# Two bias tiles of each width in the attention of a decoder trunk, the wide ones in the norms' tiles, and two tiles for the squares of q and k

## The chip, the cores and the metric

The kernel runs on one core of one Trainium2 chip. The metric is the device time of one execution in microseconds (us). The engines are named as the profile names them: PE (TensorE, matmuls), PEld (its weight loads), DVE (VectorE), ACT (ScalarE), POOL (GpSimd) and SP (SyncE, whose queue carries the DMAs of the weights). SBUF is the on-chip memory that all of them read and write, PSUM the banks into which PE accumulates.

## The reference, cut to what matters

The input is one sequence of 512 tokens with 1024 channels, in float32. Two layers run one after the other, each a token mixer with a residual add and then a squared-ReLU MLP with a residual add. The first mixer is a chunked gMLP; the second, around which the change lies, is an attention with 16 heads of 64 channels, normalised q and k, a forget-gate bias on the logits and a sigmoid gate on its output:

```
p = h @ w_in
q, k, v, gate, f_logit = split(p)
q = rms_norm(q, q_g);  k = rms_norm(k, k_g)            # per head
c = cumsum(log_sigmoid(f_logit + b_f), axis=tokens)    # per head
for each block i of 128 query rows, keys 0 .. (i+1)*128:
    logits = q @ k.T * Dh**-0.5 + c[query] - c[key]
    logits = where(query >= key, logits, -inf)
    o = softmax(logits) @ v
o = o * sigmoid(gate)
out = o @ w_out
```

For one head the four query blocks have 128, 256, 384 and 512 keys. The term `c[query] - c[key]`, with the causal mask in it, is what the kernel calls the bias.

## The kernel before, in words

The channels lie on the 128 partitions and the 512 tokens along the free axis. Every float32 matrix product is made of three matmuls with split operands (high by high, high by low, low by high), so each weight chunk comes from DRAM into a tile `raw`, ACT copies its high part `wh` (L85), and DVE, or POOL while the attention runs, subtracts it to get the low part `wl` (L86). The chunks are numbered (wl122 is the low part of chunk 122); `Stream` loads and splits them some chunks ahead of PE.

The stages follow each other: gMLP, first MLP, attention (from 638.6 to 934.5 us of the profiled span), second MLP. In the attention, eight pairs of heads are projected (`project`), one or two q/k/v column groups at a time, and the work of a pair's softmax (`attend(p, y)`, one generator per pair) is woven between the projection's matmuls. The order on PE is pinned by the program (`FOX_ORDER` says in which order projections, gates and output products come, and the `LAG_...` constants say how many microseconds of PE work lie between the steps of a generator). On DVE, ACT, POOL and SP the order is made when the kernel is built, by a scheduler with a time model, which sees when each tile comes free.

A pair's way, with the lines that the profile names: its q and k stand in `y`; ACT squares them into `ysq` (L725, two halves of 512), DVE sums the squares (L726), POOL raises them to -0.5 (L728, `yss`), DVE multiplies (L729). Then for each head `hd` of the pair a row of `c` is brought to all partitions (`cb`, L788), and for each of the four widths:

- POOL makes the bias tile from `cb` and `ct` (L795, `tensor_scalar`) and masks its diagonal block (L797, `affine_select`). The order listing calls the tile of head 9 and width 512 `bias9_3`.
- PE makes the logits `lg`, DVE adds the bias into `ee` and takes the row minimum `mn` (L806), ACT takes the exponential and its row sums (L807).

After the four, DVE takes the reciprocal `rc` of the sums (L809) and multiplies the four `ee` by it (L811, four instructions). PE turns `ee` into `tp`, ACT and DVE make its high and low parts `pth` (L845) and `ptl` (L846), and PE multiplies them with the values `v` into `ot` (one PSUM bank, shared by all heads). `v` comes from the projection's PSUM through ACT (L679) and DVE (L680). ACT and DVE bring `ot` into `oz` (L829, L830) and multiply it by the gate (L831); `output` multiplies `oz`'s halves with the output weights and adds the result to the residual stream `x` (L327).

Before the change each bias width has one tile, in the pool `fp`, so head `hd+1`'s bias of a width can be made once head `hd`'s L806 of that width has read it. `ysq` has one tile too. The pool `small` holds, for the four norms of the trunk, the tiles `sq` and `sqs` (512 wide, two of each; `Norm.square`), which no one uses while the attention's heads run; the norm after the attention squares `x` only at the attention's end.

Of the kernel before, what the change touches and what calls it, by code (L numbers as in the profile page):

```python
# [8 lines left out]
F32 = mybir.dt.float32  # L9
# [7 lines left out]
P = 128  # L17
D = 1024
S = 512
# [5 lines left out]
DH = 64  # L25
# [115 lines left out]
def trunk(ctx: ExitStack, tc: tile.TileContext, A, out, stages=4):  # L141
# [6 lines left out]
    small = ctx.enter_context(tc.tile_pool(name="small", bufs=2))  # L148
# [3 lines left out]
    def psA(name):  # L152
        return ps.tile([P, S], F32, tag="A", name=name, bufs=4)
# [455 lines left out]
    with ExitStack() as st:  # L609
        fs = st.enter_context(tc.tile_pool(name="fs", bufs=2))  # L610
        fp = st.enter_context(tc.tile_pool(name="fp", bufs=2))
# [16 lines left out]
        def forget(pq):  # L628

            fl = fp.tile([P, NT, H], F32, tag="fl", name="fl", bufs=1)  # L630
            for i in range(NT):
                dve.scalar_tensor_tensor(fl[:, i], pq[i][:, 3 * P : 3 * P + H], nm.rstd[:, i : i + 1], bf, op0=ALU.mult, op1=ALU.add)
            ff = fl.rearrange("p i h -> p (i h)")
            fa = fp.tile([P, NT * H], F32, tag="fa", name="fa", bufs=1)
            dve.scalar_tensor_tensor(fa, ff, -1.0, ff, op0=ALU.mult, op1=ALU.min)
            act.activation(fa, fa, AF.Exp)
            act.activation(fa, fa, AF.Ln, bias=1.0)
            dve.scalar_tensor_tensor(ff, ff, 0.0, fa, op0=ALU.min, op1=ALU.subtract)

            pre = fp.tile([P, NT, H], F32, tag="pre", name="pre", bufs=1)  # L640
            dve.memset(pre[:, 0], 0.0)
            for i in range(1, NT):
                dve.tensor_tensor(pre[:, i], pre[:, i - 1], fl[:, i - 1], op=ALU.add)
            yield LAG_FORGET, None
            pc = psD("pc")
            mm(pc[:, : NT * H], tri, ff, True, False)
            mm(pc[:, : NT * H], ones, pre.rearrange("p i h -> p (i h)"), False, True)
            dve.tensor_scalar(ct.rearrange("p i h -> p (i h)"), pc[:, : NT * H], -1.0, None, op0=ALU.mult)
            yield LAG_PT, None
            pt = psD("pct")  # L650
            for i in range(NT):
                turn(pt[:H, i * P : (i + 1) * P], ct[:, i])
            cs = fp.tile([H, S], F32, tag="oz", name="cs")
            act.activation(cs, pt[:H], AF.Copy, scale=-1.0)
            nc.sync.dma_start(cd, cs)
            did.add("F")
# [5 lines left out]
        def columns(pq, n):  # L662
            for c in range(4):
                wh, wl = (t[:, : 2 * n].rearrange("p (k n) -> p k n", k=2) for t in ws.take())
                for i in range(NT):
                    for kk in range(2):
                        k = 2 * c + kk
                        sl = slice(i * P, (i + 1) * P)
                        mm3(pq[i][:, :n], nm.h[k][:, sl], nm.l[k][:, sl], wh[:, kk], wl[:, kk], k == 0, k == KB - 1)
                        yield c, i, kk  # L670
# [23 lines left out]
        def project(p, values=True):  # L694
            pq = [psA(f"pq{p}_{i}") for i in range(NT)]
            for c, i, kk in columns(pq, (3 if values else 2) * P + (H if p == 0 else 0)):
                yield None
                if i < NT - 1 or not kk:
                    continue
                if p == 0 and c == 0:  # L700
                    nm.finish()
                if p == 0 and c == 1:
                    nm.spread()
            if p == 0:
                dve.tensor_scalar(epsr, nm.ms, RMS_EPS, None, op0=ALU.mult)
                running.append([order["us"], forget(pq), None])
                advance(True)
                gates[0] = gate_act(0, gates[0])
                did.add(("G", 0))
            if p:  # L710
                yield ("Q", p - 1)
            if values and p > 2:
                yield ("O", p - 3, 1)
            y = fp.tile([P, NT, 2 * P], F32, tag="y", name=f"y{p}", bufs=1)
            for i in range(NT):
                act.activation(y[:, i], pq[i][:, : 2 * P], AF.Copy)
            if values:
                keep_values(p, pq, 2 * P)
            yf = y.rearrange("p i n -> p (i n)")
            yh = yf.rearrange("p (a d) -> p a d", d=DH)  # L720
            ss = fs.tile([P, NT, 4], F32, tag="yss", name=f"yss{p}")
            sf = ss.rearrange("p i a -> p (i a)")
            for c in range(2):
                sq = fp.tile([P, 8, DH], F32, tag="ysq", name=f"ysq{p}_{c}", bufs=1)
                act.activation(sq.rearrange("p a d -> p (a d)"), yf[:, c * S : (c + 1) * S], AF.Square)  # L725
                dve.tensor_reduce(sf[:, 8 * c : 8 * c + 8], sq, axis=AX.X, op=ALU.add)  # L726
            dve.scalar_tensor_tensor(ss, ss, 1.0 / DH, epsr.unsqueeze(2).to_broadcast([P, NT, 4]), op0=ALU.mult, op1=ALU.add)
            pool.tensor_tensor(sf, sf, mhalf, op=ALU.pow)  # L728
            dve.tensor_tensor(yh, yh, sf.unsqueeze(2).to_broadcast([P, NT * 4, DH]), op=ALU.mult)  # L729
            running.append([order["us"] + LAG_NORM, attend(p, y), None])  # L730

        def gate_act(p, pg):
            gt = fp.tile([P, S], F32, tag="gt", name=f"gt{p}")
            dve.tensor_tensor(gt, pg, nm.rbc, op=ALU.mult)
            act.activation(gt, gt, AF.Sigmoid)
            return gt
# [24 lines left out]
        def attend(p, y):  # L761
# [21 lines left out]
            for e in range(2):  # L783
                hd = 2 * p + e
                yield lag, ("T", p - 1, e) if p else "F"
                lag = 0.0
                cb = fp.tile([P, S], F32, tag="cb", name=f"cb{hd}")
                nc.sync.dma_start(cb, cd[hd].partition_broadcast(P))  # L788
                ees = []
                sm = fs.tile([P, NT], F32, tag="sm", name=f"sm{hd}")  # L790
                mn = fs.tile([P, NT], F32, tag="mn", name=f"mn{hd}")
                for i in range(NT):
                    n = (i + 1) * P
                    bi = fp.tile([P, n], F32, tag=f"bias{i}", name=f"bias{hd}_{i}", bufs=1)
                    pool.tensor_scalar(bi, cb[:, :n], 1.0, ct[:, i, hd : hd + 1], op0=ALU.mult, op1=ALU.add)  # L795
                    dg = bi[:, i * P :]
                    pool.affine_select(dg, dg, pattern=[[-1, P]], compare_op=ALU.is_ge, fill=BIG, base=0, channel_multiplier=1)  # L797
                    yield lag, None
                    lag = LAG_LOGIT * rush
                    ee = fp.tile([P, n], F32, tag=f"ee{i}", name=f"ee{hd}_{i}", bufs=2)  # L800
                    ees.append(ee)
                    lg = psB(f"lg{hd}_{i}")
                    ts_ = slice(i * P, (i + 1) * P)
                    mm(lg[:, :n], qs[e][:, ts_], ks[e][:, :n], True, False)
                    mm(lg[:, :n], qs[e][:, ts_], kl[e][:, :n], False, True)
                    dve.tensor_tensor_reduce(ee, lg[:, :n], bi, 1.0, 3.0e38, op0=ALU.add, op1=ALU.min, accum_out=mn[:, i : i + 1])  # L806
                    act.activation(ee, ee, AF.Exp, bias=mn[:, i : i + 1], scale=-1.0, accum_out=sm[:, i : i + 1])  # L807
                rc = fs.tile([P, NT], F32, tag="rc", name=f"rc{hd}")
                dve.reciprocal(rc, sm)  # L809
                for i in range(NT):  # L810
                    dve.tensor_scalar(ees[i], ees[i], rc[:, i : i + 1], None, op0=ALU.mult)  # L811
                soft.append(ees)
                did.add(("L", p, e))
# [19 lines left out]
            for e in range(2):  # L833
                hd = 2 * p + e
# [4 lines left out]
                for j in range(NT):  # L839
                    n = (NT - j) * P  # L840
# [28 lines left out]
        def advance(force):  # L869

            can = [r for r in running if r[2] is None or r[2] in did]
            due = [r for r in can if r[0] <= order["us"]]
            if not due and force and can:
                due = [min(can, key=lambda r: r[0])]
                order["us"] = max(order["us"], due[0][0])
            if not due:
                return False
            r = due[0]
            try:
                lag, r[2] = next(r[1])  # L880
                r[0] = order["us"] + lag
            except StopIteration:
                running.remove(r)
            return True
# [94 lines left out]
```

## Time and profile before

| | us |
|---|---|
| median of 3 runs | 1291.09 (1291.02 to 1291.13) |
| the profiled execution, its own time | 1290.49 |
| its span in the trace | 1288.8 |
| PE busy in the span | 1263.7 (98%) |
| DVE busy | 887.4 (69%) |
| ACT busy | 631.0 (49%) |
| POOL busy | 503.4 (39%) |

The profiled execution is 0.60 us below the median and has 1.7 us outside the span. The granted clock of PE was 0.994 of full speed over the span. Times below are microseconds from the span's start. "busy" of PE counts its matmuls; a bracket behind a row of a timeline tells how long the engine had been idle and which instruction released it.

### The profile page before, as it was taken

The numbers are of one execution on the slowest core, as the hardware profiler recorded it, in microseconds if no ns is written. First come the engines' busy times: TensorE is split into PE (matmuls) and PEld (weight loads), VectorE is DVE, ScalarE is ACT, GpSimd is POOL, SyncE is SP. The second block draws the span as 40 slices with busy tenths as digits, with TensorE's granted clock in tenths as the row PEclk, the third lists the DMA queues.
The fourth block names the chain that finished last, engine by engine and source line by source line (L and its number), as shares of the span: only waits on it lengthen the run. The fifth ranks groups of instructions, "written<-read, shape, count | busy, mean of one in ns | idle before, by whom it ended". The sixth has DMA issues, their size and how long they took to land.

```text
span 1288.8 us, 18536 instructions
## 1 busy us (share of the span) xinstructions
PE 1263.7 (98%) x7180; PEld 1118.5 (87%) x7180; DVE 887.4 (69%) x1212; ACT 631.0 (49%) x993; POOL 503.4 (39%) x423
## 2 busy tenths in 40 slices
PE   9999999998999999999999999999979999999998
PEld 8888888887999999998899899898869999999987
DVE  7347766688767676765536777777897867676763
ACT  7334333355534343443467687678465434444430
POOL 4209423027423232210657667666284422222200
PEclk9999999998999999999999999999989999999999
DMA  7332323222332333323223222223213333232321
GB/s 249 95 115 82 91 90 85 96 83 70 105 121 85 112 95 102 104 94 95 80 83 99 82 83 74 87 78 106 77 64 116 99 98 107 90 114 83 115 82 66
DMA packets 39608, 124.02 MB, mean 96 GB/s; under 512 B 4816, under 2 KB 5840, under 8 KB 39520
## 3 DMA queue, kind: packets, MB, share of 16 engines
q1 hardware_dynamic: 39232, 122.82, 30.4%
q8 instruction: 56, 0.92, 0.3%
q14 instruction: 32, 0.26, 0.1%
q10 hardware_dynamic: 288, 0.02, 0.0%
HBM read 120.69 MB, written 2.13 MB: 95 GB/s over the span
## 4 chain that ended last, share of the span: by engine, by line
PE 85%; DVE 8%; ACT 2%; POOL 2%; issue 1%; DMA 1%; POOLq 0%; ACTq 0%; DVEq 0%
PE po L245 34%; PE da L245 12%; PE bc L245 9%; PE pq L245 8%; PE pv L245 7%; PE pu L245 7%; DVE xl L273 2%; PE pg L245 2%; PE ot L245 2%; DVE wl L86 1%; DVE ee L811 1%; PE lg L245 1%; PE tp L250 1%; PE sp L428 1%; ACT wh L85 1%
## 5 line engine op out<-in xcount | busy, mean ns | idle before, releaser
L85 ACT ACTIVATE wh<-raw 128x1024 fp32r<-128x1024 f32 (+3 forms) x230 | 219.0, 953 | 276.6 <-PE po L245 86.5
L86 DVE TENSOR_TENSOR wl<-raw,wh 128x1024 fp32r<-128x1024 f32 (+1 forms) x178 | 255.0, 1444 | 50.9 <-ACT wh L85 50.5
L245 PE MATMUL po<-zl,wh 128*128 128x512 f32 x512 | 200.5, 392 | 0.0
L245 PE MATMUL po<-zh,wh 128*128 128x512 f32 x512 | 200.2, 391 | 0.0
L245 PE MATMUL po<-zh,wl 128*128 128x512 f32 x512 | 199.5, 390 | 0.0
L559 DVE TENSOR_TENSOR x<-x,po 128x512 f32<-128x512 f32 x128 | 87.3, 682 | 111.5 <-PE po L245 111.5
L86 POOL TENSOR_TENSOR wl<-raw,wh 128x768 fp32r<-128x768 f32 (+3 forms) x52 | 103.1, 1983 | 124.2 <-ACT wh L85 121.7
L112 POOL TENSOR_TENSOR ssum<-raw 128x512 f32<-128x512 f32 x28 | 40.7, 1453 | 261.1 <-DMA raw<-in_m_dram 242.4
L85 ACT ACTIVATE sh<-ssum 128x1024 fp32r<-128x1024 f32 x56 | 59.4, 1061 | 169.5 <-POOL ssum L113 121.7
L245 PEld LDWEIGHTS po<-zh,wl 128*128 128x128 f32 x512 | 96.2, 188 | 19.6
L245 PEld LDWEIGHTS po<-zh,wh 128*128 128x128 f32 x512 | 96.5, 188 | 18.0
L245 PEld LDWEIGHTS po<-zl,wh 128*128 128x128 f32 x512 | 96.6, 189 | 16.2
L245 PE MATMUL pq<-wh,xh 128*128 128x384 f32 (+2 forms) x256 | 88.4, 345 | 0.0
L412 POOL TENSOR_SCALAR vn<-v,mv,lnr 128x128 f32<-128x128 f32 x64 | 63.3, 1004 | 59.4 <-DVE vl L416 59.3
L245 PE MATMUL pq<-wh,xl 128*128 128x384 f32 (+2 forms) x256 | 83.1, 324 | 0.0
L245 PE MATMUL pq<-wl,xh 128*128 128x384 f32 (+2 forms) x256 | 82.7, 323 | 0.0
L86 DVE TENSOR_TENSOR sl<-ssum,sh 128x1024 fp32r<-128x1024 f32 x56 | 71.5, 1277 | 11.5 <-ACT sh L85 11.5
L114 POOL TENSOR_TENSOR ssum<-raw,ssum 128x512 f32<-128x512 f32 x28 | 39.3, 1404 | 75.7 <-DVE sl L86 75.4
L115 POOL TENSOR_TENSOR ssum<-raw,raw 128x512 f32<-128x512 f32 x28 | 63.5, 2269 | 1.2 <-DVE sl L86 1.2
L245 PE MATMUL da<-th,sl 128*128 128x256 f32 x224 | 63.4, 283 | 0.0
L245 PE MATMUL da<-tl,sh 128*128 128x256 f32 x224 | 63.4, 283 | 0.0
L245 PE MATMUL da<-th,sh 128*128 128x256 f32 x224 | 63.1, 282 | 0.0
(212 smaller groups left out, 3517.9 us busy)
## 6 DMA issues: line engine op xcount, KB each, us to landing
raw<-in_m_dram SPq DMA_DIRECT2D x128, 512.0 KB, 3.6
raw<-in_gw_u_dram SPq DMA_DIRECT2D x16, 512.0 KB, 3.5
raw<-in_gw_o_dram SPq DMA_DIRECT2D x16, 512.0 KB, 3.5
raw<-in_fw_qkv_dram SPq DMA_DIRECT2D x20, 384.0 KB, 3.0
raw<-in_gw_v_dram SPq DMA_DIRECT2D x14, 512.0 KB, 3.8
raw<-in_fw_g_dram SPq DMA_DIRECT2D x8, 512.0 KB, 3.4
cb<-cd SPq DMA_DIRECT2D x16, 256.0 KB, 3.3
raw<-in_fw_o_dram SPq DMA_DIRECT2D x8, 512.0 KB, 3.5
```

What stands on the lines that cost most here:

```text
L85: self.nc.scalar.activation(hi, t, AF.Copy)
L86: eng.tensor_tensor(lo, t, hi.bitcast(F32), op=ALU.subtract)
L112: tt(s12[:, 0], a21, a22, op=ALU.add)
L114: tt(s43[:, 0], a12, s12[:, 1], op=ALU.subtract)
L115: tt(s43[:, 1], a11, a21, op=ALU.subtract)
L245: ins = pe.matmul(dst, a, b, start=start, stop=stop, skip_group_check=more)
L250: placed(pe.transpose(dst, src, ident[: src.shape[0], : src.shape[0]]), 256)
L273: dve.scalar_tensor_tensor(l, x[b], gcol, h.bitcast(F32), op0=ALU.mult, op1=ALU.subtract)
L412: pool.tensor_scalar(vn[:, i], v[i][:, cb * P : (cb + 1) * P], mv[:, i, 0:1], lnr[:, i : i + 1], op0=ALU.subtract, op1=ALU.mult)
L428: pe.matmul(dst, vh[:, 2 * c + i], wide, start=True, stop=False)
L559: dve.tensor_tensor(x[b], x[b], pt, op=ALU.add)
L811: dve.tensor_scalar(ees[i], ees[i], rc[:, i : i + 1], None, op0=ALU.mult)
```

## The change

`ysq` gets two tiles instead of one. The biases of the two narrow widths get two tiles each in the pool `fp`; the biases of the two wide widths leave `fp` and use the norms' `sqs` and `sq` (two of each), cut to the width. The bytes per partition of the pools stay the same in sum (1536 and 2048 leave `fp`; 512, 1024 and 2048 come). The lines behind L794 move down by four, so L795 is L799 in the changed kernel, L806 is L810, L811 is L815.

```
-                sq = fp.tile([P, 8, DH], F32, tag="ysq", name=f"ysq{p}_{c}", bufs=1)
+                sq = fp.tile([P, 8, DH], F32, tag="ysq", name=f"ysq{p}_{c}", bufs=2)
...
-                    bi = fp.tile([P, n], F32, tag=f"bias{i}", name=f"bias{hd}_{i}", bufs=1)
+
+                    if i < 2:
+                        bi = fp.tile([P, n], F32, tag=f"bias{i}", name=f"bias{hd}_{i}", bufs=2)
+                    else:
+                        bi = small.tile([P, S], F32, tag="sqs" if i == 2 else "sq", name=f"bias{hd}_{i}", bufs=2)[:, :n]
                     pool.tensor_scalar(bi, cb[:, :n], 1.0, ct[:, i, hd : hd + 1], op0=ALU.mult, op1=ALU.add)
```

No instruction is added or removed. PE's order and the order of the DMAs on SP stay as they were; the scheduler places work on the other three engines anew. On POOL it differs at the first four heads, at heads 9 and 10, and at the end.

POOL at the attention's start, before: the four biases of head 0, then the weight split wl122, and head 1's biases one by one behind it.

```order
L797 AFFINE_SELECT bias0_0_5952<-bias0_0_5952 128x128
L797 AFFINE_SELECT bias0_1_5966<-bias0_1_5966 128x128
L797 AFFINE_SELECT bias0_2_5989<-bias0_2_5989 128x128
L86 TENSOR_TENSOR wl122_5927<-raw122_5747,wh122_5926 128x768
L797 AFFINE_SELECT bias0_3_6006<-bias0_3_6006 128x128
L795 TENSOR_SCALAR bias1_0_6039<-cb1_6035,ct_5603 128x128
L86 TENSOR_TENSOR wl123_5977<-raw123_5821,wh123_5976 128x768
L797 AFFINE_SELECT bias1_0_6039<-bias1_0_6039 128x128
```

The same place in the changed kernel:

```order
L801 AFFINE_SELECT bias0_0_5952<-bias0_0_5952 128x128
L799 TENSOR_SCALAR bias1_0_6039<-cb1_6035,ct_5603 128x128
L799 TENSOR_SCALAR bias1_1_6053<-cb1_6035,ct_5603 128x256
L799 TENSOR_SCALAR bias1_2_6076<-cb1_6035,ct_5603 128x384
L801 AFFINE_SELECT bias0_1_5966<-bias0_1_5966 128x128
L799 TENSOR_SCALAR bias1_3_6093<-cb1_6035,ct_5603 128x512
L801 AFFINE_SELECT bias0_2_5989<-bias0_2_5989 128x128
L86 TENSOR_TENSOR wl122_5927<-raw122_5747,wh122_5926 128x768
L801 AFFINE_SELECT bias0_3_6006<-bias0_3_6006 128x128
L801 AFFINE_SELECT bias1_0_6039<-bias1_0_6039 128x128
```

All four L799 of head 1 now stand ahead of the masks of head 0's last three biases and of wl122; behind the last row come three more masks of head 1, with one L799 of head 2 among them, and then wl123.

POOL at the attention's end, before: head 15's biases stand among the splits wl158 to wl161.

```order
L86 TENSOR_TENSOR wl158_8660<-raw158_8448,wh158_8659 128x1024
L795 TENSOR_SCALAR bias15_0_8772<-cb15_8768,ct_5603 128x128
L795 TENSOR_SCALAR bias15_1_8786<-cb15_8768,ct_5603 128x256
L797 AFFINE_SELECT bias15_0_8772<-bias15_0_8772 128x128
L795 TENSOR_SCALAR bias15_2_8809<-cb15_8768,ct_5603 128x384
L86 TENSOR_TENSOR wl159_8710<-raw159_8517,wh159_8709 128x1024
L797 AFFINE_SELECT bias15_1_8786<-bias15_1_8786 128x128
L797 AFFINE_SELECT bias15_2_8809<-bias15_2_8809 128x128
L795 TENSOR_SCALAR bias15_3_8826<-cb15_8768,ct_5603 128x512
L86 TENSOR_TENSOR wl160_8794<-raw160_8599,wh160_8793 128x1024
L797 AFFINE_SELECT bias15_3_8826<-bias15_3_8826 128x128
L86 TENSOR_TENSOR wl161_8881<-raw161_8657,wh161_8880 128x1024
```

The same place in the changed kernel:

```order
L86 TENSOR_TENSOR wl156_8520<-raw156_8287,wh156_8519 128x512
L728 TENSOR_TENSOR yss7_8506<-yss7_8506,mhalf_120 128x16
L86 TENSOR_TENSOR wl157_8602<-raw157_8364,wh157_8601 128x512
L86 TENSOR_TENSOR wl158_8660<-raw158_8448,wh158_8659 128x1024
L86 TENSOR_TENSOR wl159_8710<-raw159_8517,wh159_8709 128x1024
L86 TENSOR_TENSOR wl160_8794<-raw160_8599,wh160_8793 128x1024
L86 TENSOR_TENSOR wl161_8881<-raw161_8657,wh161_8880 128x1024
```

Head 15's biases are all made ahead of wl156, and the splits follow each other without a bias between them.

DVE at the attention's end, before: behind the four L811 of head 14 (its row of width 256 of head 15's logits comes first), the values v6 and v7 and head 15's last logits.

```order
L806 ISA ee15_1_8803,mn15_8771<-lg15_1_8804,bias15_1_8786 128x256
L806 ISA mn15_8771 128x1
L680 SCALAR_TENSOR_TENSOR v6_8855<-pv3_0_8595,rstd2_5678,v6_8855 128x128
L806 ISA ee15_2_8820,mn15_8771<-lg15_2_8821,bias15_2_8809 128x384
L806 ISA mn15_8771 128x1
L680 SCALAR_TENSOR_TENSOR v6_8855<-pv3_1_8596,rstd2_5678,v6_8855 128x128
L680 SCALAR_TENSOR_TENSOR v6_8855<-pv3_2_8597,rstd2_5678,v6_8855 128x128
L680 SCALAR_TENSOR_TENSOR v7_8867<-pv3_0_8595,rstd2_5678,v7_8867 128x128
```

The same place in the changed kernel:

```order
L810 ISA ee15_1_8803,mn15_8771<-lg15_1_8804,bias15_1_8786 128x256
L810 ISA mn15_8771 128x1
L810 ISA ee15_2_8820,mn15_8771<-lg15_2_8821,bias15_2_8809 128x384
L810 ISA mn15_8771 128x1
L680 SCALAR_TENSOR_TENSOR v6_8855<-pv3_0_8595,rstd2_5678,v6_8855 128x128
L680 SCALAR_TENSOR_TENSOR v6_8855<-pv3_1_8596,rstd2_5678,v6_8855 128x128
L810 ISA ee15_3_8837,mn15_8771<-lg15_3_8838,bias15_3_8826 128x512
L810 ISA mn15_8771 128x1
```

Head 15's two wide logits have moved ahead of values.

A little later on DVE, in the changed kernel:

```order
L813 RECIPROCAL rc15_8843<-sm15_8770 128x4
L327 TENSOR_TENSOR x0_87<-x0_87,po159_0_8884 128x512
L815 TENSOR_SCALAR ee15_0_8780<-ee15_0_8780,rc15_8843 128x128
L815 TENSOR_SCALAR ee15_1_8803<-ee15_1_8803,rc15_8843 128x256
L815 TENSOR_SCALAR ee15_2_8820<-ee15_2_8820,rc15_8843 128x384
L815 TENSOR_SCALAR ee15_3_8837<-ee15_3_8837,rc15_8843 128x512
L680 SCALAR_TENSOR_TENSOR v7_8867<-pv3_2_8597,rstd2_5678,v7_8867 128x128
L680 SCALAR_TENSOR_TENSOR v7_8867<-pv3_3_8598,rstd2_5678,v7_8867 128x128
L834 TENSOR_TENSOR oz6_8529<-ot12_8864,oz6_8529 64x512
```

Before, v7's last two rows and oz6 stood directly behind x0, ahead of rc15 and the four L811 of head 15; now they stand behind them.

## Rows read from the trace of the kernel before

**Rows 1.** Busy time by engine in the attention: stretch, length, engines, clock, DMA.
```profile
638.60:934.50 295.90, 288.64 (x1722) 263.74 (x1722) 206.52 (x464) 209.02 (x431) 180.15 (x188) 1.00 0.29 86
```

**Rows 2.** What PE waited for in 640 to 934: total us, times, longest.
```profile
PE tp L250 <- DVE ptl L846: 5.1, 4, 1.9
```

**Rows 3.** Timeline of PE: start, duration, line, operation, tiles, idle before and releaser.
```profile
692.00 0.33 PE L250 MATMUL tp<-ident,ee 128*128 128x128 f32 x1 [1.95 <-DVE ptl L846]
...
894.91 0.50 PE L245 MATMUL ot<-pth,v 128*128 128x512 f32 x1 [0.63 <-DVE v L680]
...
901.04 0.40 PE L245 MATMUL ot<-pth,v 128*128 128x512 f32 x1
```

**Rows 4.** DVE's waits in the attention: total us, times, longest.
```profile
DVE ee L806 <- POOL bias L797: 1.9, 2, 1.3
```

**Rows 5.** Groups by line in the attention: ACT's squares.
```profile
L725 ACT ACTIVATE ysq<-y 128x512 f32<-128x512 f32 x16 | 10.1, 632 | 0.1
```

**Rows 6.** Timeline of DVE, 806 to 813.
```profile
807.23 1.27 DVE L811 TENSOR_SCALAR ee<-ee,rc 128x128 f32<-128x128 f32 x4
...
811.83 0.69 DVE L806 CUSTOM_DVE_ANT_0 ee<-lg,bias 128x512 f32<-128x512 f32 x1 [0.55 <-POOL bias L797]
```

**Rows 7.** Timeline of POOL, heads 0 to 3, and beside the 807.23 above.
```profile
672.76 2.08 POOL L795 TENSOR_SCALAR bias<-cb,ct 128x128 f32<-128x128 f32 x4 [4.68 <-DVE kl L778]
...
675.54 1.87 POOL L86 TENSOR_TENSOR wl<-raw,wh 128x768 fp32r<-128x768 f32 x1
677.35 0.31 POOL L797 TENSOR_SCALAR_AFFINE_SELECT bias<-bias 128x128 f32<-128x128 f32 x1
677.62 0.39 POOL L795 TENSOR_SCALAR bias<-cb,ct 128x128 f32<-128x128 f32 x1
...
688.37 1.84 POOL L86 TENSOR_TENSOR wl<-raw,wh 128x768 fp32r<-128x768 f32 x1 [0.38 <-ACT wh L85]
...
807.11 2.91 POOL L728 TENSOR_TENSOR yss<-yss,mhalf 128x16 f32<-128x16 f32 x1
```

**Rows 8.** Timeline of DVE, 679 to 692.
```profile
679.04 0.69 DVE L806 CUSTOM_DVE_ANT_0 ee<-lg,bias 128x512 f32<-128x512 f32 x1 [0.59 <-PE lg L245]
...
681.00 2.10 DVE L811 TENSOR_SCALAR ee<-ee,rc 128x128 f32<-128x128 f32 x4
...
687.54 2.95 DVE L811 TENSOR_SCALAR ee<-ee,rc 128x128 f32<-128x128 f32 x4
```

**Rows 9.** Timeline of POOL, 890 to 901.
```profile
890.25 2.41 POOL L86 TENSOR_TENSOR wl<-raw,wh 128x1024 fp32r<-128x1024 f32 x1 [0.70 <-ACT wh L85]
...
893.94 2.54 POOL L86 TENSOR_TENSOR wl<-raw,wh 128x1024 fp32r<-128x1024 f32 x1
...
897.88 2.40 POOL L86 TENSOR_TENSOR wl<-raw,wh 128x1024 fp32r<-128x1024 f32 x1 [1.15 <-ACT wh L85]
```

**Rows 10.** Timeline of ACT, 891 to 900.
```profile
891.88 1.04 ACT L85 ACTIVATE wh<-raw 128x1024 fp32r<-128x1024 f32 x1
...
896.74 1.06 ACT L85 ACTIVATE wh<-raw 128x1024 fp32r<-128x1024 f32 x1
...
898.85 0.71 ACT L807 ACTIVATE ee<-ee,mn 128x512 f32<-128x512 f32 x1
```

**Rows 11.** Timeline of DVE, 892 to 900.
```profile
892.21 2.04 DVE L811 TENSOR_SCALAR ee<-ee,rc 128x128 f32<-128x128 f32 x4
...
894.52 0.34 DVE L680 SCALAR_TENSOR_TENSOR v<-pv,rstd,v 128x128 fp32r<-128x128 f32 x1
...
894.78 0.54 DVE L806 CUSTOM_DVE_ANT_0 ee<-lg,bias 128x384 f32<-128x384 f32 x1
...
898.18 0.69 DVE L327 TENSOR_TENSOR x<-x,po 128x512 f32<-128x512 f32 x1 [0.34 <-PE po L245]
898.79 0.60 DVE L680 SCALAR_TENSOR_TENSOR v<-pv,rstd,v 128x128 fp32r<-128x128 f32 x2
899.31 0.67 DVE L830 TENSOR_TENSOR oz<-ot,oz 64x512 f32<-64x512 f32 x1
```

## The prediction, made before the changed kernel's time was known

> **What bounds the kernel now.** I read the busy time by stage first. In the attention PE is busy for 288.64 of 295.90 us at the full granted clock, column PEclk 1.00, the 2.4 GHz level [rows 1]; no other engine comes near that. The change touches no other stage, so what it can move is the rest, some 7 us, and whatever makes that rest longer. The waits of PE come next. The largest entry is `tp` waiting for `ptl`, 5.1 us in 4 waits, the longest 1.9 [rows 2]: PE wants to turn a head's probabilities, and DVE is late with the softmax chain of the head before. The timeline of PE gives the places. I use three: the stall of 1.95 before the turn at 692.00 (heads 0 and 1), the stall of 0.63 before `ot12` at 894.91, which waits for the values v6, and the start of `ot13` at 901.04, which does not stall but shares one PSUM bank with `ot12` [rows 3].
>
> What the change addresses is seen in two other views. DVE waited for a bias 1.9 us in 2 waits in the whole attention [rows 4], and none of PE's three places above is released by one. The largest that I could place is 0.55 at 811.83, head 9's width of 512 [rows 6]. For `ysq`, ACT was idle ahead of its squares 0.1 us in total [rows 5]. So the second tiles have almost no wait to remove, and their effect has to come through the new order on POOL and DVE.
>
> **The change part by part.** No instruction is added or removed, so no work gets longer by itself.
>
> `ysq`: at most the 0.1 us of [rows 5] goes, and that wait is on ACT, beside PE; I take 0.
>
> Where the biases are made one head ahead and nothing else in their order changes, which holds from head 4 to head 8 and from there until wl155, the cost is 0 as well: the same instructions and the same splits pass in the same sequence, and DVE hardly waited for either.
>
> Head 9 (about 808 to 818): the wait of 0.55 goes [rows 6], but PE has no stall there that it ended; in exchange the four L811 of head 9 now stand ahead of two residual adds. I take 0, between 0 and +0.7 (about half of the 1.27 that now stands ahead of the adds; how much room they have no row shows).
>
> Before the two places that cost, one thing that the trace shows of DVE beside POOL. The four L811 of a head are the same work each time. They took 1.27 at 807.23 while POOL ran the power `yss` from 807.11 on [rows 6, 7]. They took 2.10 at 681.00, beside POOL's bias rows, and 2.95 at 687.54, when the split of 688.37 (1.84) fell on their last part [rows 7, 8]; and 2.04 at 892.21, beside the split that began at 890.25 and ends at 892.66 [rows 9, 11]. So who stands beside them on POOL is worth up to 2.95 - 1.27 = 1.68 us.
>
> The Trainium skill states a rule on this, in SBUF — State Buffer, section Who interferes with whom: VectorE and GpSimd share a port pair under an exclusive lock, whoever issues first keeps it for the whole instruction and the other fully blocks. The trace's 2.95 against 1.27 agrees with that; by it alone a split of 2.4 us that begins in the middle of the four L811 would cost them all 2.4, while a mere slowdown as at 681.00 would cost 0.83, and the sum below would then be 1.6 lower in its second term.
>
> **Heads 0 and 1.** Before, POOL makes head 0's biases (2.08 for four L795), then masks and wl122 (1.87), and the last mask of head 0 ends at 677.35 + 0.31 = 677.66 [rows 7]. Now the four L795 of head 1, again 2.08, stand ahead of it: 679.74. DVE's L806 of that tile began at 679.04, released by the logits [rows 8], so it begins 0.70 later, and with it the reciprocal and head 0's four L811: 681.00 becomes 681.70.
>
> Behind that mask POOL now has three more masks of head 1 (0.31 each), one L795 (0.39), another mask and then wl123: 679.74 + 0.93 + 0.39 + 0.31 = 681.4, or 681.2 as POOL's rows overlap a little, so wl123 runs from 681.2 to 683.1. It falls on head 0's four L811. If they are blocked until 683.1 and take 1.27 to 1.8 after that, they end at 684.4 to 684.9 instead of 681.00 + 2.10 = 683.10: 1.3 to 1.8 late. I take 1.5.
>
> All of head 1 follows in DVE's order, so its four L811 begin at 687.54 + 1.5 = 689.04. What they take there sets the stall at 692.00. Free, 1.27, they end at 690.3, 0.2 before the 690.49 of now; beside bias rows, 2.10, at 691.15, 0.65 later; again 2.95, at 692.0, 1.5 later; with the whole split behind them 2.3. POOL will be at head 2's and head 3's biases then, as it was beside 681.00, so I take **+0.65**, between -0.2 and +2.3. Nothing hides it: PE is already waiting at that turn.
>
> **The end.** Before, wl160 stood behind head 15's last bias and began at 893.94 [rows 9]. With the biases gone from its way it begins when its high part is there, 891.88 + 1.04 = 892.92 [rows 10], say 893.0. The L811 of head 14 begin at 892.21 as before and end at 894.25 now [rows 11]; the split that was beside them has ended by 892.66, so two of the four are done when wl160 takes over for 2.4 until 895.4. The other two then end at about 895.9, +1.65. Behind them the order has head 15's L806 of width 384 ahead of v6's first row, 0.54 more [rows 11]: v6 comes 1.65 + 0.54 = **2.2** later, and `ot12` at 894.91 waits for it [rows 3]. If nothing blocks, it is 0.5 alone.
>
> Then `ot13`. It began at 901.04 and would now begin at 901.04 + 2.2 = 903.25; its bank is free when DVE's add of `ot12` into `oz` is done, which before ran 899.31 to 899.98, a margin of 1.06. Now the four L811 of head 15 and their reciprocal stand ahead of that add. Their exponential follows the high part of chunk 161, 896.74 + 1.06 = 897.80, on ACT; delayed by the same 2.2 less its slack I put it at 899.6, it ends with its row sums at 900.5 [rows 10]. Reciprocal 0.2 and x0 0.69 give 901.4 [rows 11]; four L811 at 1.27 give 902.7, or 903.4 if wl161 (2.40) stands beside them until 902.2; v7's two rows 0.60 and the add 0.69 give 904.0 or 904.7. Against 903.25 that is +0.75 or +1.45; I take **+1.5**, since these two L811 groups have had a split beside them in the nearest rows. The end as a whole: 3.7, between 0.5 and 4.
>
> **The sum.** 0.65 + 3.7 + 0 = 4.35, against the profiled execution's 1290.49 (span 1288.8 and 1.7 around it): 1294.84. The median of the runs stands 0.60 above the profiled execution, so 1295.4.
>
> **The rivals.**
> Nothing catches. The change doesn't do what it says: there was no wait for biases worth the name, POOL and DVE meet as often as before, only elsewhere, and only the order itself costs: 0.7 at the start at most half of which reaches PE (0.35), 0.5 for the moved L806 and 0.75 for `ot13`: +1.6, so 1292.7. For it speaks that PE's stalls are few [rows 2]; against it, that the two blocked places lie right where PE waits.
>
> Heavier. Head 1's four L811 meet a whole split (+2.3), the end costs 3.85, head 9's add 0.3: +6.4, 1297.5. For it speaks 2.95 at 687.54 [rows 8]; against it that wl125 now stands behind head 3's biases, which wait for head 1's last L806.
>
> The other side, faster by a little. That same order is the mechanism: the split that blocks head 1's four L811 now, at 688.37 [rows 7], can't begin before head 3's last bias is made, which needs head 1's L806 of width 512 read and two L795 and masks made, so not before about 690. If head 0's delay stays under about 1.1 (wl123 not catching its L811), head 1's four L811 begin before 688.7 and are free: 2.95 - 1.27 = 1.68 less, and at the end POOL's last bias row no longer meets head 14: 0.2 to 0.3 less. That is -1.9, 1289.2. It decides by whether head 0 is late by less than 1.1; against it, POOL's wl123 falls right on head 0 by the sum above.
>
> **How the numbers follow.** A difference of 0.2%, 2.6 us, is about what a measurement of this kernel can tell from no change, so "same" is 1288.5 to 1293.7. The chances: my forecast 0.50 (1295.4; by its own bounds an eighth of it lies below 1293.7), nothing catches 0.22 (1292.7, nearly all same, an eighth slower), heavier 0.13, the other side 0.15 (1289.2, of which half, 0.07, goes past 1288.5). That gives faster 0.07, same 0.06 + 0.19 + 0.08 = 0.33, slower 0.60. The range reaches from 1290.6, below the case in which nothing catches, to 1298.8, above the heavier one with the upper end 4 at the end of the attention; the other side is what it leaves out. The likeliest case's own range is 1293 to 1297.
>
> **What would show it.** In the changed profile: the stall before head 1's first turn, 1.95 now, at 2.6; head 0's four L811 longer than 2.10, with wl123 beside them; head 14's longer than 3, with wl160 beginning at about 893; the stall before `ot12` at about 2.8; and a new stall of about 1.5 before `ot13`, released by the add into `oz`. The forecast is wrong if head 14's four stay near 2 us, or if the turn of head 1 comes earlier than 692, or if PE loses time between 700 and 880, where I put nothing.

## The result, and the profile after

The changed kernel took 1299.09 us (median of 6 runs, 1295.33 to 1302.05) against 1291.11 us (6 runs, 1290.56 to 1291.93): a ratio of 1.0059, 95% interval 1.0048 to 1.0070, so 7.6 us slower by the ratio (8.0 between the two medians). Forecast were 4.3 us slower, 1295.4; the measured time lies at the upper end of the forecast range, 1298.8 (0.3 above it by the median, just inside it by the ratio). The profiled execution took 1298.86 us, with a span of 1297.1.

What PE waited for, in the whole span after (total us, times, longest):

```profile
PE tp L250 <- DVE ptl L850: 5.2, 4, 1.9
PE ot L245 <- DVE v L680: 2.7, 1, 2.7
PE pq L245 <- DVE v L680: 2.5, 1, 2.5
```

The waits for `ptl` are as large as before [rows 2]. `ot` waits 2.7 instead of 0.63 [rows 3], and a wait of 2.5 is new. The timeline of PE after gives their places:

```profile
689.72 0.45 PE L245 MATMUL pq<-wh,xh 128*128 128x384 f32 x1 [2.47 <-DVE v L680]
...
696.29 0.33 PE L250 MATMUL tp<-ident,ee 128*128 128x128 f32 x1 [1.94 <-DVE ptl L850]
...
900.82 0.79 PE L245 MATMUL ot<-pth,v 128*128 128x512 f32 x1 [2.69 <-DVE v L680]
...
908.12 0.50 PE L245 MATMUL ot<-pth,v 128*128 128x512 f32 x1
```

Set against [rows 3], the same matmuls start 4.29, 5.91 and 7.08 us later (the last three rows). PE was 1.30 behind at its first turn in the attention, before any instruction that the change moves; first before, then after:

```profile
669.22 0.66 PE L250 MATMUL tq<-ident,y 128*128 128x128 f32 x4 [0.74 <-DVE y L729]
```

```profile
670.52 0.66 PE L250 MATMUL tq<-ident,y 128*128 128x128 f32 x4 [0.74 <-DVE y L729]
```

So heads 0 and 1 cost 4.29 - 1.30 = 2.99; from there to `ot12` another 1.62 (0.31 came back near 822), and from `ot12` to `ot13` 1.17. The 1.2 that is left to the 8.3 of the spans comes behind the attention.

So 5.8 of the 8.3 lie where the change moves instructions. The 1.30 ahead of it differs from execution to execution: the same first turn stands at 670.05 in the profile of change_again, which is the same kernel once more, at 669.40 in one_ysq and at 671.06 in start_exact, and up to there all these kernels do the same work in the same order (the runs are described below). The 5.8 alone do not explain that the times differ by as much as 7.6.

**Heads 0 and 1.** DVE after, around head 0's normalisations (the four L811 of before are L815 now; a row with x4 merges the four widths and shows the first one's shape):

```profile
680.85 0.69 DVE L810 CUSTOM_DVE_ANT_0 ee<-lg,bias 128x512 f32<-128x512 f32 x1 [1.09 <-POOL bias L801]
...
682.77 6.29 DVE L815 TENSOR_SCALAR ee<-ee,rc 128x128 f32<-128x128 f32 x4
...
693.51 1.27 DVE L815 TENSOR_SCALAR ee<-ee,rc 128x128 f32<-128x128 f32 x4
```

They took 6.29 us, not 2.10 [rows 8]. Grouped by shape, 682.7 to 689.1 (busy us, mean ns, idle before), three of the four were caught:

```profile
L815 DVE TENSOR_SCALAR ee<-ee,rc 128x384 f32<-128x384 f32 x1 | 2.6, 2561 | 0.0
L815 DVE TENSOR_SCALAR ee<-ee,rc 128x128 f32<-128x128 f32 x1 | 2.3, 2314 | 0.0
L815 DVE TENSOR_SCALAR ee<-ee,rc 128x256 f32<-128x256 f32 x1 | 1.1, 1145 | 0.0
L815 DVE TENSOR_SCALAR ee<-ee,rc 128x512 f32<-128x512 f32 x1 | 0.5, 506 | 0.0
```

POOL in the same stretch ran from wl123 to wl124 without a pause:

```profile
682.11 1.86 POOL L86 TENSOR_TENSOR wl<-raw,wh 128x768 fp32r<-128x768 f32 x1
683.93 1.06 POOL L799 TENSOR_SCALAR bias<-cb,ct 128x256 f32<-128x256 f32 x2
684.93 0.31 POOL L801 TENSOR_SCALAR_AFFINE_SELECT bias<-bias 128x128 f32<-128x128 f32 x1
685.23 1.16 POOL L799 TENSOR_SCALAR bias<-cb,ct 128x512 f32<-128x512 f32 x2
686.36 1.81 POOL L86 TENSOR_TENSOR wl<-raw,wh 128x768 fp32r<-128x768 f32 x1
```

The first normalisation ends only when wl123 and both L799 behind it are done, the second spans the next mask and two L799, the third wl124 and the masks behind it. Behind them on DVE stands `v` (L680), which frees PE's projection banks: hence the new stall at 689.72.

**The end.** DVE's four and POOL's wl160 after:

```profile
896.05 3.63 DVE L815 TENSOR_SCALAR ee<-ee,rc 128x128 f32<-128x128 f32 x4
```

```profile
896.84 2.56 POOL L86 TENSOR_TENSOR wl<-raw,wh 128x1024 fp32r<-128x1024 f32 x1 [0.34 <-ACT wh L85]
```

wl160 begins as soon as its high part is there and catches the last of head 14's four. Then PE's clock falls. Windows of one microsecond after (stretch, length, engines, then the granted clock as the third number from the end):

```profile
900.00:901.00 1.00, 0.18 (x1) 0.18 (x2) 1.00 (x7) 0.94 (x4) 0.00 (x0) 0.88 0.62 102
901.00:902.00 1.00, 1.00 (x3) 0.81 (x4) 1.00 (x5) 1.00 (x5) 0.00 (x0) 0.50 0.91 360
902.00:903.00 1.00, 1.00 (x5) 0.81 (x4) 0.67 (x3) 1.00 (x3) 0.00 (x0) 0.50 0.16 61
903.00:904.00 1.00, 1.00 (x5) 0.81 (x4) 0.04 (x1) 1.00 (x4) 0.70 (x1) 0.50 0.00 0
```

Behind the idle 2.69 us PE runs three microseconds at 0.50, the 1.2 GHz level; that makes most of the 1.17 between `ot12` and `ot13`.

### The profile page after: what moved, and what is told of

It reads as the page before. It is cut to its first block, busy times and chain, and to the rows that moved or that the text cites. A ratio compares the mean times of both kernels' runs of the same rounds, so it can differ in the third digit from the quotient of the medians.

```text
span 1297.1 us, 18509 instructions
## 1 busy us (share of the span) xinstructions
PE 1267.5 (98%) x7180; PEld 1121.4 (86%) x7180; DVE 891.6 (69%) x1212; ACT 630.7 (49%) x993; POOL 501.6 (39%) x423
## 4 chain that ended last, share of the span: by engine, by line
PE 86%; DVE 7%; ACT 2%; POOL 2%; issue 1%; DMA 1%; POOLq 0%; ACTq 0%; DVEq 0%
PE po L245 34%; PE da L245 12%; PE bc L245 9%; PE pq L245 8%; PE pv L245 7%; PE pu L245 7%; PE pg L245 2%; DVE xl L273 2%; PE ot L245 2%; PE lg L245 1%; DVE wl L86 1%; DVE ee L815 1%; PE tp L250 1%; PE sp L428 1%; ACT wh L85 1%
```

## The experiments

They were timed in three groups, each in turn with the kernel before on one chip (its medians there 1291.47, 1291.64 and 1291.69). The last two columns are the time of four normalisations in the one profiled execution of each run.

| run | median us (runs) | ratio, 95% interval | head 0's four | head 14's four |
|---|---|---|---|---|
| one_ysq | 1296.56 (6) | 1.0045, 1.003 to 1.006 | 2.89 | 3.62 |
| start_order | 1297.56 (6) | 1.0049, 1.0034 to 1.0063 | 4.93 | 3.62 |
| end_order | 1293.90 (9) | 1.0022, 1.0011 to 1.0034 | 6.30 | 2.04 |
| one_port | 1295.58 (5) | 1.0033, 1.0021 to 1.0045 | 1.94 | 1.95 |
| start_exact | 1295.94 (5) | 1.0033, 1.002 to 1.0045 | 2.08 | 3.63 |
| both_exact | 1292.33 (11) | 1.0009, 1.0 to 1.0018 | 2.23 | 2.04 |
| before_port | 1291.08 (11) | 0.9998, 0.9989 to 1.0007 | 1.94 | 1.95 |
| after_port | 1292.48 (11) | 1.0006, 0.9998 to 1.0015 | 1.94 | 1.95 |
| wide_alone | 1298.89 (5) | 1.0056, 1.0043 to 1.0069 | 2.52 | 3.77 |
| change_again | 1298.37 (5) | 1.0054, 1.004 to 1.0068 | 6.31 | 3.63 |
| one_row | 1291.86 (11) | 0.9998, 0.9989 to 1.0006 | 2.17 | 2.04 |
| row_and_port | 1288.91 (11) | 0.9983, 0.9974 to 0.9992 | 2.23 | 2.04 |

The theory: POOL rows that follow each other without a gap keep DVE's normalisations out. The rivals: the moved work itself, a slowdown instead of a block, the clock, the second `ysq` tile.

**Parts of the change.** one_ysq and change_again:

```
-                sq = fp.tile([P, 8, DH], F32, tag="ysq", name=f"ysq{p}_{c}", bufs=2)
+                sq = fp.tile([P, 8, DH], F32, tag="ysq", name=f"ysq{p}_{c}", bufs=1)
```

> The change with one tile for the squares instead of two; the order on every engine is that of the change. Theory: the second tile for the squares is worth nothing, so 1299 us as the change, head 0's four normalisations again at about 6.3 us and head 14's at 3.6. Rival: the second tile takes part in the loss or hides some of it, then the time is off 1299 by more than 1 us. The spread of its runs also shows whether the change's 1295 to 1302 is its own.

> The change itself once more. Theory (head 0's normalisations are caught by POOL's rows in some executions and not in others, the end is lost in all): its runs fall into two groups, near 1295 and near 1299, as the six runs with one tile for the squares did, with a median between 1295 and 1299. Rival (one broad distribution, or a second tile for the squares that adds to the loss): no gap between 1296 and 1298, or nearly all runs near 1299 as in the first six.

In one_ysq's profile head 0's first normalisation waited only until wl123 had ended. DVE, then POOL there:

```profile
681.41 1.28 DVE L815 TENSOR_SCALAR ee<-ee,rc 128x128 f32<-128x128 f32 x1
```

```profile
680.76 1.85 POOL L86 TENSOR_TENSOR wl<-raw,wh 128x768 fp32r<-128x768 f32 x1
682.60 1.07 POOL L799 TENSOR_SCALAR bias<-cb,ct 128x256 f32<-128x256 f32 x2
```

The order is that of the change, and the normalisation begins 0.65 behind wl123's start, as in the change (0.66). In one execution DVE gets in when the split ends (1.28), in the other not until two more rows have passed (2.31). In one_ysq's profile the start then cost PE nothing, since head 1's four, behind which the turn near 692 waits, were shorter than the 2.95 of before [rows 8]. DVE and PE there:

```profile
688.74 1.91 DVE L815 TENSOR_SCALAR ee<-ee,rc 128x128 f32<-128x128 f32 x4
```

```profile
692.15 0.33 PE L250 MATMUL tp<-ident,ee 128*128 128x128 f32 x1 [1.88 <-DVE ptl L850]
```

The turn is 0.15 later than in [rows 3], and PE was 0.18 late already at its first turn. With this order at the start, the profiles of the change, of change_again and of end_order show 6.29, 6.31 and 6.30 and that of one_ysq alone 2.89. So the place is one source of the spread of the runs; how much of it, the runs without a profile don't tell. one_ysq's median missed the 1299 that I expected. The two groups that I expected are not there: one_ysq has 1294.2 to 1294.9 and 1298.3 to 1299.7, but change_again has 1296.93 and 1297.71 too. Whether the second `ysq` tile shifts the odds (1296.56 against 1298.37 and 1299.09) stays open; 6 runs against 11 don't settle it.

wide_alone gives two tiles to the wide widths only; the narrow ones and `ysq` keep one:

```
                     if i < 2:
-                        bi = fp.tile([P, n], F32, tag=f"bias{i}", name=f"bias{hd}_{i}", bufs=2)
+                        bi = fp.tile([P, n], F32, tag=f"bias{i}", name=f"bias{hd}_{i}", bufs=1)
```

> The part of the change on the two wide widths alone: they use the norms' tiles, the narrow widths and the squares keep one tile. POOL has wl160 right behind wl159 and the last narrow mask, ahead of which head 15's wide biases are long made. Theory: wl160 catches head 14's last normalisation as in the change (3.6 us), the end loses 4.5 us, and at the start head 0 may be caught or not: 1295.5 to 1299. Rival (the loss comes from the narrow tiles or from all together): 1292.

The wide half alone loses as much as the whole change. At the end head 14's third is the one caught, 2.62 of the 3.77. At the start it loses elsewhere: head 0's four took 2.52, head 1's 2.71, and PE then stood 3.64 before the turn near 692. The narrow half alone was not tried.

**POOL's order put back.** start_order, start_exact, end_order and both_exact are the change with edges of issue order on POOL (one instruction is issued only behind another), of this kind (start_exact):

```
+HOLD = {(1, 0, 0): ((0, 3, 1),), (1, 0, 1): (123,), (1, 1, 0): (123, (1, 0, 1)), ...
...
+                            for h in HOLD.get((hd, i, k), ()):
+                                held.enter_context(tc.issue_after(ws.made[h]))
```

> The change, with POOL's order in heads 1 and 2 held as before (head 1's and head 2's biases behind wl122, wl123 and wl124 again); DVE's and ACT's orders are those of the change. Theory (POOL instructions that follow each other without a gap keep DVE out): head 0's four normalisations fall from 6.3 us to about 2.1, the stall of 2.5 us before the projection's matmul near 690 goes, and the time is 3 us lower, 1296. Rival (the moved work on DVE and ACT, or only the end, makes the loss): 1299.

> The change, with head 15's biases held among wl158 to wl160 as before; DVE's and ACT's orders at the end go back with them. Theory: head 14's normalisations take about 2.0 us instead of 3.6, the stall before ot12 is 0.6 instead of 2.7, the half clock that follows it (about 1.2 us of the loss) goes too, and the time is 3 us lower, 1296. Rival (the half clock comes from elsewhere or from the stall at the start): 1298 at best, with the clock still at half after 901.

> The change, with POOL's rows held word for word as before from head 0 up to head 3's first biases (the earlier attempt left four bias rows in a run, and head 0's normalisations still took 4.9 us); the end stays as in the change. Theory: head 0's four take about 2.1 us, head 1's about 3, there is no stall near 690, the end still costs 3 us: 1294 to 1295.5. Rival (the place is not what matters, head 0 is blocked whatever the order): 1297 or more.

> The change, with POOL's order held as before at the start (as in start_exact) and at the end (head 15's biases among wl158 to wl160). Theory: both losses go, head 0's four 2.1 us and head 14's 2.0: 1291 to 1292, as before, although every bias keeps its second tile. Rival (a third loss, or one from the tiles' places in memory): 1294 or more.

start_order missed: 1297.56, not 1296. It had brought wl123 back but left four L799 in a run behind it, and head 0 was blocked by these, the masks and wl124. DVE, then POOL there:

```profile
681.50 4.93 DVE L818 TENSOR_SCALAR ee<-ee,rc 128x128 f32<-128x128 f32 x4
```

```profile
680.13 2.07 POOL L801 TENSOR_SCALAR bias<-cb,ct 128x256 f32<-128x256 f32 x4
682.16 0.79 POOL L804 TENSOR_SCALAR_AFFINE_SELECT bias<-bias 128x128 f32<-128x128 f32 x3
682.91 1.85 POOL L86 TENSOR_TENSOR wl<-raw,wh 128x768 fp32r<-128x768 f32 x1
```

With the rows word for word as before (start_exact) head 0 takes 2.08, and the five runs lie within 0.7 us of each other, where the change's eleven spread over 6.7. (both_exact, with the same rows held, spreads over 3.9 in eleven runs, so five may be too few.) DVE and ACT keep the change's order in heads 0 and 1 here, so POOL's order alone makes the block of head 0. I had expected 3 us for head 1's four; they took 1.28. What is left, 1.0033, is the end and a loss in heads 2 and 3 that both_exact has too. In its profile the stall before `ot12` is that of the change, but the clock stayed at 1.00 behind it, and PE then did wait for `oz`. PE and the clock:

```profile
898.95 0.50 PE L246 MATMUL ot<-pth,v 128*128 128x512 f32 x1 [2.69 <-DVE v L681]
...
906.06 0.50 PE L246 MATMUL ot<-pth,v 128*128 128x512 f32 x1 [0.69 <-DVE oz L840]
```

```profile
899.00:903.00 4.00, 3.62 (x17) 2.83 (x18) 2.64 (x10) 3.98 (x12) 1.57 (x1) 1.00 0.28 110
```

end_order does the opposite, with head 14 at 2.04 and head 0 at 6.30; its median, 1293.90, is 2 us below what I expected. Here the scheduler put DVE's and ACT's rows at the end back nearly as before too, so this run does not separate them from POOL's; one_port and after_port, below, do. both_exact undoes both, and with two tiles for every bias it is 0.09% from before. It isn't the old order everywhere: against before, the stall near 692 is 1.6 shorter in its profile, and heads 2 and 3, beside POOL rows that now stand elsewhere, lose 2.0 between 718 and 728. Near 692 POOL's rows do stand as before, and what differs is who came first by hundredths of a microsecond. DVE, then POOL of both_exact:

```profile
687.94 1.28 DVE L821 TENSOR_SCALAR ee<-ee,rc 128x128 f32<-128x128 f32 x4
```

```profile
688.77 2.14 POOL L87 TENSOR_TENSOR wl<-raw,wh 128x768 fp32r<-128x768 f32 x1 [0.74 <-ACT wh L86]
```

Here the last of head 1's four began 0.03 ahead of the split, took 0.48, and the split paid (2.14, not 1.84). Before, the split at 688.37 [rows 7] began 0.01 ahead of the last of the four, which then took 2.11 of their 2.95 [rows 8]. How often before loses this race, the runs without a profile don't tell. Apart from such places the tiles cost nothing that these runs show; the order that they let the scheduler choose does.

**The form of the normalisation.** one_port leaves the change's order nearly as it is (one exchange on POOL, a few on DVE and ACT) and writes the normalisations of heads 0 and 14 so that they also accumulate a row sum (`ee` stays what it is; the remark on it in the expectation was wrong):

```
-                    dve.tensor_scalar(ees[i], ees[i], rc[:, i : i + 1], None, op0=ALU.mult)
+                    dve.tensor_scalar(ees[i], ees[i], rc[:, i : i + 1], None, op0=ALU.mult, op1=ALU.add, accum_out=un[:, i : i + 1])
```

> The change, with the normalisation of heads 0 and 14 written as multiply, add and accumulate over the row (its outputs ee are wrong, the row sum is added in a tile that no one reads): the same instructions in nearly the same order on the same engine, in a form that VectorE runs at one element per cycle. Theory (an exclusive lock of the ports that the fast form takes): head 0's and head 14's four take about 2 us each whatever POOL runs beside them, and the time falls by 5 to 6 us to 1293 to 1294. Rival (POOL's traffic slows everything on DVE, or the order makes the loss): they stay at 6 and 3.6 us or more, 1299.

Both heads take 1.94 and 1.95, with wl123 and wl160 beside them as in the change. The time fell by less than forecast, since the block moved on: head 1, in the old form, met wl125 and the bias rows. DVE and PE there:

```profile
689.91 4.19 DVE L819 TENSOR_SCALAR ee<-ee,rc 128x128 f32<-128x128 f32 x4
```

```profile
695.34 0.33 PE L250 MATMUL tp<-ident,ee 128*128 128x128 f32 x1 [3.73 <-DVE ptl L854]
```

before_port and after_port use the form in heads 0, 1, 2, 10, 13 and 14.

> The kernel before, with the normalisations of heads 0, 1, 2, 10, 13 and 14 in the accumulating form that took 1.95 us beside a split. POOL's order is that of before. Theory: the form is safe from POOL but slower when POOL is quiet, so the four take 1.95 instead of 2.10, 2.95, 2.75, 2.42, 2.40 and 2.04; the stalls before the turns near 692, 722 and 875 fall by 1.0, 0.8 and 0.4: 1288.9. Rival (those stalls are set by other steps of the chain): 1291.

> The change with the same six heads in the accumulating form. Theory: without the lock at the two places the change costs what its order costs alone, 0.7 to 1.1 for head 0's late bias and about 1.7 at the end (as in one_port, where PE waited 1.0 and 1.3 for v there), less 1.0, 0.8 and 0.4 gained at the three stalls: 1291 to 1292; and its runs lie as close together as those of before (3 us at most), since the lottery between POOL and DVE is what spreads them. Rival (the spread is the clock's, or the loss moves on to the next head): 1294 or more, spread over 5 us.

after_port's 24 such instructions (duration in ns: least, median, most) vary with their width alone (0.34, 0.47 to 0.48, 0.61 and 0.74 us for the four widths):

```profile
L817 DVE TENSOR_SCALAR_CACHE_REDUCE ee<-ee,rc x24: 342/543/744, 682.7 to 894.6; 128x128 f32<-128x128 f32 x6, 128x256 f32<-128x256 f32 x6, 128x384 f32<-128x384 f32 x6, 128x512 f32<-128x512 f32 x6
```

It keeps the change's order on POOL but for one exchange and is level with before, within 2.1 us from run to run, so most of the loss was the block. The moved work has a price too: set against before_port, which has the same form in the same heads, after_port is 1.4 us slower, and PE waits longer for the values `v` at the end, though head 14's four took 1.95. Those waits in after_port's attention, where before had only the 0.63 of [rows 3]:

```profile
PE po L245 <- DVE v L680: 1.3, 1, 1.3
PE ot L245 <- DVE v L680: 1.0, 1, 1.0
```

one_port has the same two waits. Compared with before matmul by matmul, PE lost 1.5 us between 882 and `ot13` in after_port and 3.2 in the change. So a little under half of the end's loss is the new order by itself, and the rest is the block of head 14. before_port's gain was not found in the times: 1291.08, where I had expected 1288.9.

**One row moved, and a version faster than both.** one_row is the kernel before with wl125 behind `yss1` on POOL; row_and_port adds the accumulating form for heads 2 and 13:

```
-            pool.tensor_tensor(sf, sf, mhalf, op=ALU.pow)
+            power = pool.tensor_tensor(sf, sf, mhalf, op=ALU.pow)
+            if p == 1:
+                ws.behind[125] = tc.issue_after(power.ins)
```

> The kernel before with one row of POOL moved: wl125 behind the power yss1 instead of ahead of it; nothing else in any order changes. Theory: head 1's four normalisations, 2.95 us before since wl125 caught the last of them, take 1.27; the stall of 1.95 before the turn near 692 falls to 0.3, as it did in start_exact; wl125 is then 6.7 us later and still in time for PE. 1289.8. Rival (PE would wait for wl125, or the stall is set elsewhere): 1291.5 or more.

> As one_row, and the normalisations of heads 2 and 13 in the accumulating form (1.95 us, against 2.75 and 2.40 now). Theory: the stalls before the turns near 722 and 875 fall by 0.8 and 0.45 as in before_port: 1288.6, faster than both kernels. Rival (the gains are given back later, as the median of before_port, 1291.1, may say): 1291.

In one_row head 1 takes 1.28 and the stall of 1.95 falls to 0.34, as expected, but the time does not. PE, then the clock by windows:

```profile
690.96 0.33 PE L251 MATMUL tp<-ident,ee 128*128 128x128 f32 x1 [0.34 <-DVE ptl L849]
...
721.46 0.30 PE L251 MATMUL tp<-ident,ee 128*128 128x128 f32 x1 [1.90 <-DVE ptl L849]
```

```profile
722.00:726.00 4.00, 4.00 (x19) 3.78 (x19) 3.76 (x5) 1.70 (x5) 1.47 (x1) 0.59 0.34 96
```

Behind the next stall, 1.90, the clock went to 0.59 over four microseconds; before, the same stall of 1.90, ended at 722.52, left it at 1.00:

```profile
722.00:726.00 4.00, 2.78 (x18) 2.42 (x19) 4.00 (x6) 2.71 (x5) 2.54 (x3) 1.00 0.18 30
```

In this execution that gave back half of the gain; whether it does so in all of them no run shows. row_and_port shortens that stall too. Its waits of PE in the attention:

```profile
PE tp L251 <- DVE ptl L853: 2.5, 4, 1.1
...
PE ot L246 <- DVE v L681: 0.6, 1, 0.6
```

2.5 us instead of 5.1 [rows 2], and at 1288.91 it is 0.17% faster than before (0.08 to 0.26) and 9.5 us faster than the change as timed beside it (change_again).

## Why the prediction was right in kind and short in size

The prediction had the kind of loss and both places right. That the total came out near the upper end of the range, and not beyond it, is in part luck: the first place cost far more than its term, the second about its term but partly by the clock, and 2.6 of the 8.3 between the spans stand outside the attention, where the prediction had put nothing.

- **That the tiles have no wait to remove:** right. both_exact, with the tiles and the old order at the two places, is level with before.
- **The end, forecast 3.7, measured 3.2 (between 882 and `ot13`):** right in its first term. Head 14's four took 3.63, `ot12`'s stall is 2.69 against the forecast 2.8, and `ot12` came 2.1 later against 2.2. The second term came near its 1.5 by luck: `ot13` did not wait for its bank in the change, because PE came at half clock and so 1.17 later; where the clock held (start_exact) it waited 0.69 and came 0.98 later than `ot12` did.
- **Heads 0 and 1, forecast +0.65, measured 2.99:** the mis-sized term. The step was "If they are blocked until 683.1 and take 1.27 to 1.8 after that". It held in one_ysq's execution (2.89, ended 684.3, forecast 684.4 to 684.9), though there the start cost nothing and not 0.65, since head 1's four took 1.91 and not 2.10; and it failed in the change's: I let DVE through when the split had ended, but POOL's next rows were already there, and each of three normalisations waited again (they took 2.31, 1.15 and 2.56).
- **Where the loss would show:** wrong. I put it in the stall before the turn near 692, which stayed at 1.94. It stood 6.6 us earlier, in the projection's matmul that waits for `v` behind the normalisations.
- **Head 9, forecast 0:** 0.31 came back a little behind it, near 822; why was not looked into.
- **The rivals:** the heavier one, 1297.5, was nearer in time than my own case, but not by its steps: head 1's four met no whole split in the change. That nothing catches is refuted by 6.29 and 3.63; its 1.6 for the order alone is near the 1.4 of after_port over before_port. The other side's mechanism was real in one point: with wl125 behind head 3's first biases no split held up head 1's four, and not only because head 0 had held everything up, for in one_ysq, where it hardly had, they took 1.91 and not 2.95.
- **The clock** was in no term: a stall of 2.69 was followed by three microseconds at the 1.2 GHz level.
- **Outside the attention**, where the prediction had no term: 1.30 ahead of it and 1.2 behind it. The 1.30 is the execution's and not the change's, by the 0.18 of one_ysq; for the 1.2 that stays open.

The Trainium skill, SBUF — State Buffer, section Who interferes with whom, leaves the form of `tensor_scalar` that also writes out its accumulator out of the instructions that can contend with GpSimd for the shared port pair. The runs agree: 1.94 and 1.95 for that form beside wl123 and wl160, against 6.29 and 3.63 for the plain one.

## What to carry to other kernels

A second buffer is not only a wait less: it lets a scheduler pack an engine's work tighter, and tight rows on POOL can shut DVE out of work that PE needs, as they did here. When an order changes, look which DVE instructions on the critical chain now fall beside a dense run on POOL, and price them by the whole run, not by one instruction. A critical normalisation is safer in a form that POOL did not block in any of these runs, but only where POOL is busy: it cost 1.95 against 1.27 free.

## What the runs showed of the hardware that I had not expected

- With the same order and the same lead of 0.65 us, a normalisation waited 1.28 in one execution and 2.31 in another: who comes next after a POOL instruction was not fixed.
- Not every POOL row blocks. The power `yss` ran for 2.91 us beside head 8's four, and they took 1.27, as little as anywhere [rows 6, 7]. The rows that held DVE up here are the splits and the runs of bias rows.
- A multiply with two SBUF inputs, `y` (L729) of pair 4, took 1.22 in the change and 3.50 in after_port, where PE then waited 1.77 at the turn near 789.6. The Trainium skill, SBUF — State Buffer, section Who interferes with whom, says that DVE instructions with two SBUF inputs contend with POOL's reads; these durations agree, though no run was made to isolate it. DVE, POOL and PE of after_port:

```profile
785.44 3.50 DVE L729 TENSOR_TENSOR y<-y,yss 128x1024 f32<-128x1024 f32 x1
```

```profile
785.47 2.39 POOL L86 TENSOR_TENSOR wl<-raw,wh 128x1024 fp32r<-128x1024 f32 x1
```

```profile
789.60 0.33 PE L250 MATMUL tp<-ident,ee 128*128 128x128 f32 x1 [1.77 <-DVE ptl L854]
```

- In the change `y` and the split met as well, but there `y` began 0.07 ahead and the split paid, 3.41 instead of 2.39; in start_order, where the split began 0.07 ahead, `y` paid again, 3.41. After_port's two starts lie too close (0.03) to tell who came first. DVE and POOL, first of the change, then of start_order:

```profile
789.55 1.22 DVE L729 TENSOR_TENSOR y<-y,yss 128x1024 f32<-128x1024 f32 x1
789.62 3.41 POOL L86 TENSOR_TENSOR wl<-raw,wh 128x1024 fp32r<-128x1024 f32 x1
```

```profile
788.51 2.39 POOL L86 TENSOR_TENSOR wl<-raw,wh 128x1024 fp32r<-128x1024 f32 x1
788.58 3.41 DVE L729 TENSOR_TENSOR y<-y,yss 128x1024 f32<-128x1024 f32 x1
```

- A stall of PE was sometimes followed by microseconds at half clock and sometimes not. Behind 1.90 near 722 the clock was 1.00 before and 0.59 over four microseconds in one_row; behind 2.69 before `ot12` it was 0.50 in the change and 1.00 in start_exact.
